# Conv module of a streaming encoder: 35 packs of taps on TensorE for 31, and another order of the steps

## The chip, the cores and the metric

The kernel runs on one core of a Trainium2 chip. The metric is the device time of one execution, in microseconds (us). Before the change three runs took 2794.42, 2795.19 (the median) and 2796.18 us.

In the views of the profile, PE is TensorE's matmuls and PEld its weight loads, DVE is VectorE, ACT is ScalarE, POOL is GpSimd, and SP is the engine whose queue issues nearly all DMAs (SPq in rows).

## The reference

One inference step of an encoder of four layers, for a prompt of 512 rows and a sample of 64, 1024 channels. Each layer has a token mixer and then a convolutional feed-forward part; the mixer of layer 1 is the convolution module, and only there does the change lie.

```python
def _dwconv(xp, w, b):
    y = lax.conv_general_dilated(xp, w[:, None, :], (1,), 'VALID',
                                 dimension_numbers=('NWC', 'WIO', 'NWC'),
                                 feature_group_count=xp.shape[-1])
    return y + b

def _conv_module(h, state, w_pw1, b_pw1, w_dw, b_dw, ln_g, ln_b, w_pw2, b_pw2):
    a, g = jnp.split(h @ w_pw1 + b_pw1, 2, axis=-1)
    glu = a * jax.nn.sigmoid(g)
    xp = jnp.concatenate([state, glu], axis=1)
    c = jax.nn.silu(_layernorm(_dwconv(xp, w_dw, b_dw), ln_g, ln_b))
    return c @ w_pw2 + b_pw2, xp[:, -(CONV_WIDTH - 1):]

# in _trunk, for layer i:
#   x = x + _rmsnorm(y, g[1])              y of the mixer
#   y, s = _conv_ffn(h, st, ...)           ConvFFN: up, conv of width 3, gate, down
```

`CONV_WIDTH` is 31: each channel of the depthwise convolution is a sum of 31 shifted rows, each with a weight of its own (a tap).

## The kernel before, in words

Channels lie on the partitions, in eight tiles of 128; the 576 rows of prompt and sample lie along the free axis. A pointwise product is done as three passes of PE (high part by high part, high by low, low by high; lines 287 to 289), so each weight is loaded by SP (512 KB), cast by ACT (L256) and its low part made by DVE (`v_w_l`, L259). Rows are worked on in two parts, `hf` 0 and 1, of 256 and 320 columns.

In the module each tile goes through these steps. PE makes the four products of pw1 (`v_p`, two for the values and two for the gate). DVE turns them into scaled rows (`v_t`, L1320), ACT takes the sigmoid, DVE gates (`v_glu`, L1329). Then the 31 taps: a number of them in packs of four on PE, one on ACT (L1394), the rest on DVE, one instruction over 128x606 each (`v_cv`, L1396). For the packs the tile's gated rows are first copied to four tiles `v_g` (L1374), one for each group of 32 channels, with the four shifts beside each other; DVE makes diagonal weights (`v_dg`, L1381); and a pack is eight matmuls (L1405, 16 records in the trace) into two cuts of 256 and 350 columns. Three matmuls close the sum with the mean `v_about` (L1412 to 1414). The join (`v_d`, L1421) adds the two parts on DVE; ACT squares; PE sums rows and squares over the channels (`v_sums`, L1450). Behind the last sums come the statistics and the second pointwise product (pw2), whose weights are loaded in the stage too.

`CPACKS` gives the packs of each tile. The order of ACT, DVE, POOL and PE in the stage is written out by hand in the string `CORDER`: each word is a step and a tile, and a third sign repeats it. `do()` plays the words in turn:

- x: a quarter of a tile's product; t, i, g: turn, sigmoid, gate;
- C: the four copies; y: diagonals; e: one pack; w: the closing matmuls;
- b: the first tap outside the packs, on ACT; d: one tap on DVE; j: the join; z, q: squares and sums;
- H, h, l: load, cast and low part of a pw1 weight; W, O, o: the same for pw2;
- R: steps of the input's norm; r, v: state rows; m, n, u: centring; K: a table of ACT.

SP is not in the string. Its order is set by the scheduler, from when the buffers of its loads come free.

The constants of the module come in earlier, while the feed-forward part of layer 0 ends: `columns` (L200 to 227) loads rows by SP to a stage tile, transposes them on PE and copies them from PSUM by ACT. Among them are the packs' columns, 32 small loads. Where the loads stand in SP's order, other loads wait behind them, such as `f_d`, the down-projection's weights of that feed-forward part.

Of the kernel before, what the change touches and what calls it, by code (L numbers as in the profile page):

```python
# [17 lines left out]
P = 128  # L18
# [5 lines left out]
NF = 22  # L24
NEG = -1.0e30
APART = 1
CPACKS = (5, 4, 4, 4, 4, 4, 3, 3)

CORDER = (
# [8 lines left out]
)  # L38

AORDER = (  # L40
# [92 lines left out]
def encoder_step_kernel(  # L133
# [12 lines left out]
    V, S, G, T = nc.vector, nc.scalar, nc.gpsimd, nc.tensor  # L146

    def pool(name, bufs=1, **kw):
        return ctx.enter_context(tc.tile_pool(name=name, bufs=bufs, **kw))
# [6 lines left out]
    wp = pool("work", 6)  # L156
# [11 lines left out]
    def ms_tile(name):  # L168
        return msp.tile([P, 512], F32, tag="ms", name=name)
# [10 lines left out]
    def w_tile(name, shape, dt=F32):  # L180
        return wp.tile(shape, dt, tag="t", name=name)

    def dram(ap, off, dims):
        return bass.AP(ap.tensor, ap.offset + off, dims)
# [14 lines left out]
    def columns(name, pieces, n, tile_pool=None, tag="ct", bufs=2):  # L199

        pt = ms_tile(f"{name}_ps")
        ct = (tile_pool or sp).tile([P, n], F32, tag=tag, bufs=bufs, name=name)
        at, group, used, stage = 0, [], 0, None
        cuts = []
        for src, rows in pieces:
            done = 0
            while done < rows:
                take = min(rows - done, P - used)
                cuts.append((src, done, take, at, used))
                done += take  # L210
                used += take
                if used == P:
                    at, used = at + P, 0
        starts = sorted({c[3] for c in cuts})
        for a in starts:
            stage = w_tile(f"{name}_r{a}", [P, P])
            m = 0
            for src, done, take, at_, used_ in cuts:
                if at_ == a:
                    to = stage[used_ : used_ + take]  # L220
                    if len(src.shape) == 3:
                        to = to.rearrange("r (a b) -> r a b", a=src.shape[1])
                    nc.sync.dma_start(to, src[done : done + take])
                    m = max(m, used_ + take)
            T.transpose(pt[:, a : a + m], stage[:m], ident[:m, :m])
        S.copy(ct, pt[:, :n])
        return ct
# [1044 lines left out]
    def conv_module(i, j):  # L1272
        n = f"v{i}"
        rows = lambda a, k: (a[j].rearrange("(c p) -> c p", p=P), k)

        packs, at = [], 296
        four = {}
        for c, np_ in enumerate(CPACKS):
            four[c] = at
            for q in range(4):  # L1280
                at += np_
                packs.append((dram(conv_w_dw[j], c * P + q * 32, [[4 * D, np_], [D, 4], [1, 32]]), np_))
        ct = columns(f"{n}_ct", [rows(conv_b_pw1, 16), rows(conv_b_dw, 8), rows(conv_ln_g, 8), rows(conv_ln_b, 8), rows(conv_b_pw2, 8), (conv_w_dw[j].rearrange("w (c p) -> (w c) p", p=P), 248), *packs], at)
        wt = ct[:, 48:296].rearrange("p (w c) -> p w c", c=8)

        pm = w_tile(f"{n}_pm", [P, P])
        V.tensor_copy(pm.rearrange("p (r s) -> p r s", s=4), ident.rearrange("p (s r) -> p r s", s=4))
        pps = ms_tile(f"{n}_tp_ps")
        T.matmul(pps[:, : at - 296], pm, ct[:, 296:at], start=True, stop=True)
        tp = sp.tile([P, at - 296], F32, tag="tp", bufs=1, name=f"{n}_tp")  # L1290
        S.copy(tp, pps[:, : at - 296])
        stt = columns(f"{n}_st", [(state_conv[j, 0].rearrange("w (c p) -> (w c) p", p=P), 240)], 240, tag="mix").rearrange("p (w c) -> p w c", c=8)
# [58 lines left out]
        class Tile:  # L1351
# [4 lines left out]
            def __init__(self, c):  # L1356
                self.c = c
                self.m = f"{n}_{c}"
                self.packs = CPACKS[c]
                self.te = 4 * self.packs  # L1360
# [71 lines left out]
            def rows(self):  # L1432
                c, pt = self.c, self.pt
                S.copy(po[c // 2][:, :, (c % 2) * P : (c % 2 + 1) * P], pt[:30, : 2 * P].rearrange("p (a b) -> p a b", a=2))
                if c % 2:
                    for s, dst in ((0, p_conv), (1, s_conv)):
                        nc.sync.dma_start(dst[j, 0][:, (c // 2) * 256 : (c // 2 + 1) * 256], po[c // 2][:, s])
# [410 lines left out]
    for at, i in enumerate(layers):  # L1848
        mixer = (attention, conv_module, chunk_mlp)[i % 3]
        subs += [mixer(i, i // 3, *(True,) * (at == 0)), ffn(i)]  # L1850
# [57 lines left out]
```

## Time and profile before

| | |
|---|---|
| runs, median | 2795.19 us (2794.42 to 2796.18) |
| profiled execution | 2793.36 us, span 2791.6 us |
| granted clock of TensorE, mean | 0.990 |
| PE, DVE, ACT, POOL busy in the span | 98%, 67%, 41%, 14% |
| the stage of the string, 694.00 to 844.30 us | 150.30 us: PE 134.45, DVE 147.16, ACT 39.66 |

The page counts busy time over the whole span, whereas windows cut it at stated times. A timeline row is a start, a duration, an engine, a line, and the operation with what it writes and reads; x4 means four alike in a row. In brackets stands the idle time of the engine ahead of it and what released it. The clock in a window is the granted share of full speed.

### The profile page before, as it was taken

The numbers are of one execution on the slowest core, as the hardware profiler recorded it, in microseconds if no ns is written. First come the engines' busy times: TensorE is split into PE (matmuls) and PEld (weight loads), VectorE is DVE, ScalarE is ACT, GpSimd is POOL, SyncE is SP. The second block draws the span as 40 slices with busy tenths as digits, with TensorE's granted clock in tenths as the row PEclk, the third lists the DMA queues.
The fourth block names the chain that finished last, engine by engine and source line by source line (L and its number), as shares of the span: only waits on it lengthen the run. The fifth ranks groups of instructions, "written<-read, shape, count | busy, mean of one in ns | idle before, by whom it ended". The sixth has DMA issues, their size and how long they took to land.

```text
span 2791.6 us, 52728 instructions
## 1 busy us (share of the span) xinstructions
PE 2740.8 (98%) x20825; PEld 2622.4 (94%) x20825; DVE 1858.2 (67%) x4199; ACT 1137.2 (41%) x2393; POOL 386.9 (14%) x937
## 2 busy tenths in 40 slices
PE   8999999998998999999999999999999999999998
PEld 7889999998867999999999999999999879999998
DVE  5668666666994866666747657666676676766674
ACT  4655433334225543333434224432334664533243
POOL 3122111110000111111002102211110121211111
PEclk9999999999998999999999999999999999999999
DMA  6312322222641232322223221322222421322221
GB/s 166 91 48 69 99 78 90 76 64 64 151 113 40 63 105 76 90 78 92 75 80 97 78 76 55 92 84 84 82 90 61 107 57 40 106 76 86 81 84 59
DMA packets 357625, 230.69 MB, mean 83 GB/s; under 512 B 43038, under 2 KB 347906, under 8 KB 357250
## 3 DMA queue, kind: packets, MB, share of 16 engines
q1 hardware_dynamic: 357378, 227.33, 28.5%
q8 instruction: 164, 2.69, 0.4%
q14 instruction: 83, 0.68, 0.1%
HBM read 212.87 MB, written 7.45 MB: 79 GB/s over the span
## 4 chain that ended last, share of the span: by engine, by line
PE 90%; DVE 7%; DMA 1%; issue 1%; ACT 1%; SPq 0%; POOL 0%; POOLq 0%; DVEq 0%; ACTq 0%
PE f_p L287 13%; PE f_p L289 13%; PE f_p L288 13%; PE o_p L287 10%; PE o_p L288 10%; PE o_p L289 10%; DVE v_cv L1396 3%; PE m_u_p L287 1%; PE m_u_p L289 1%; PE m_u_p L288 1%; PE m_vp L287 1%; PE m_vp L288 1%; PE m_vp L289 1%; PE t_o L1178 1%; PE t_sp L1117 1%; PE t_qp L287 1%
## 5 line engine op out<-in xcount | busy, mean ns | idle before, releaser
L287 PE MATMUL f_p<-n_hi,f_w_h 128*128 128x320 f32 (+1 forms) x2688 | 799.8, 298 | 0.0
L289 PE MATMUL f_p<-n_hi,f_w_l 128*128 128x320 f32 (+1 forms) x2688 | 798.0, 297 | 0.0
L288 PE MATMUL f_p<-n_lo,f_w_h 128*128 128x320 f32 (+1 forms) x2688 | 797.9, 297 | 0.0
L287 PEld LDWEIGHTS f_p<-n_hi,f_w_h 128*128 128x128 f32 x2688 | 510.4, 190 | 4.5 <-issue 4.1
L288 PEld LDWEIGHTS f_p<-n_lo,f_w_h 128*128 128x128 f32 x2688 | 510.4, 190 | 0.0
L289 PEld LDWEIGHTS f_p<-n_hi,f_w_l 128*128 128x128 f32 x2688 | 510.4, 190 | 0.0
L287 PE MATMUL o_p<-f_ah,f_d_h 128*128 128x256 f32 (+1 forms) x1408 | 419.6, 298 | 2.2 <-ACT f_d_h L256 2.2
L288 PE MATMUL o_p<-f_al,f_d_h 128*128 128x256 f32 (+1 forms) x1408 | 418.5, 297 | 0.0
L289 PE MATMUL o_p<-f_ah,f_d_l 128*128 128x256 f32 (+1 forms) x1408 | 417.6, 297 | 0.0
L256 ACT CAST f_w_h<-f_w_f 128x512 fp32r<-128x512 f32 x352 | 200.8, 618 | 494.9 <-PE f_p L288 235.6
L537 DVE TENSOR_TENSOR o_y<-o_p,o_y 128x256 f32<-128x256 f32 (+1 forms) x432 | 195.1, 455 | 262.0 <-PE o_p L289 260.7
L800 DVE TENSOR_TENSOR f_ub<-f_p,n_R 128x256 f32<-128x256 f32 x352 | 148.3, 423 | 286.9 <-PE f_p L289 282.3
L287 PEld LDWEIGHTS o_p<-f_ah,f_d_h 128*128 128x128 f32 x1408 | 268.5, 191 | 4.0 <-ACT f_d_h L256 2.5
L288 PEld LDWEIGHTS o_p<-f_al,f_d_h 128*128 128x128 f32 x1408 | 268.6, 191 | 0.2 <-issue 0.2
L289 PEld LDWEIGHTS o_p<-f_ah,f_d_l 128*128 128x128 f32 x1408 | 268.3, 191 | 0.2 <-issue 0.2
L259 DVE TENSOR_TENSOR f_w_l<-f_w_f,f_w_h 128x512 fp32r<-128x512 f32 x352 | 229.1, 689 | 20.0 <-ACT f_w_h L256 17.9
L256 ACT CAST f_d_h<-f_d_f 128x512 fp32r<-128x512 f32 x176 | 101.3, 619 | 232.6 <-PE f_p L288 171.8
L808 POOL COPY f_fo<-f_ub 128x2 f32<-128x2 f32 x176 | 47.2, 268 | 885.7 <-DVE f_ub L800 878.8
L812 DVE SCALAR_TENSOR_TENSOR f_c<-f_ub,f_ct,f_c 128x578 f32<-128x578 f32 x176 | 144.0, 821 | 38.3 <-ACT f_c L811 38.3
L811 ACT ACTIVATE f_c<-f_ub,f_ct 128x578 f32<-128x578 f32 x176 | 150.8, 863 | 1.4 <-POOL f_fo L808 0.7
L821 ACT CAST f_ah<-f_a 128x576 fp32r<-128x576 f32 x88 | 59.2, 673 | 218.2 <-DVE f_a L818 218.2
L813 DVE SCALAR_TENSOR_TENSOR f_c<-f_ub,f_ct,f_c 128x578 f32<-128x578 f32 x176 | 143.5, 817 | 2.8
(380 smaller groups left out, 5607.6 us busy)
## 6 DMA issues: line engine op xcount, KB each, us to landing
f_w_f<-in_ffn_w_up_dram SPq DMA_DIRECT2D x176, 512.0 KB
f_d_f<-in_ffn_w_down_dram SPq DMA_DIRECT2D x80, 512.0 KB
v_w_f<-in_conv_w_pw_dram SPq DMA_DIRECT2D x24, 512.0 KB
t_wq_f<-in_attn_w_qkv_dram SPq DMA_DIRECT2D x32, 256.0 KB
t_wo_f<-in_attn_w_o_dram SPq DMA_DIRECT2D x32, 256.0 KB
m_wv_f<-in_cmlp_w_in_dram SPq DMA_DIRECT2D x16, 512.0 KB
m_u_w_f<-in_cmlp_w_in_dram SPq DMA_DIRECT2D x16, 512.0 KB
m_wo_f<-in_cmlp_w_out_dram SPq DMA_DIRECT2D x16, 512.0 KB
```

Of the source, the lines that this page charges most:

```text
L256: S.copy(hi[:, a:e], st[:, a:e])
L259: eng.tensor_tensor(lo[:, a:e], st[:, a:e], hi[:, a:e].bitcast(F32), ALU.subtract)
L287: T.matmul(ps, lh, rh, start=(i == 0), stop=False)
L288: T.matmul(ps, lh, rl, start=False, stop=False)
L289: T.matmul(ps, ll, rh, start=False, stop=(i == n - 1))
L537: V.tensor_tensor(ys, ps, ys, ALU.add)
L800: V.tensor_tensor(ub[q][:, b : b + 256], ps[q]()[:, :256], h.R[:, hf * 256 : hf * 256 + 256], ALU.mult)
L811: S.activation(y, ub[q][:, 2:580], AF.Identity, bias=ct[:, 3, c : c + 1], scale=ct[:, 2, c : c + 1])
L812: V.scalar_tensor_tensor(y, ub[q][:, 1:579], ct[:, 1, c : c + 1], y, ALU.mult, ALU.add)
L813: V.scalar_tensor_tensor(y, ub[q][:, 0:578], ct[:, 0, c : c + 1], y, ALU.mult, ALU.add)
L821: S.copy(a_hi[p], am)
L1396: V.scalar_tensor_tensor(self.cv, g, w, self.cv, ALU.mult, ALU.add)
```

## The change

- `CPACKS` becomes (5,5,5,4,4,4,4,4), which sums to 35, in place of (5,4,4,4,4,4,3,3), which sums to 31. Tiles 1, 2, 6 and 7 get one pack more, and four taps fewer on DVE: 100 in all in place of 116.
- `CORDER` is another string with the same steps except for these numbers.
- The columns of the packs no longer lie in the tile `v_ct`, which shrinks from 420 to 296 columns, but in a tile `v_ctp` of their own, 140 columns, from the work pool. There are three and two transposes in place of four, and one more copy on ACT.

```diff
-CPACKS = (5, 4, 4, 4, 4, 4, 3, 3)
+CPACKS = (5, 5, 5, 4, 4, 4, 4, 4)
 CORDER = (
...
-    "e5 o1 d4 w5 b6 y6 d6 e4 W3 j5 e4 d6 z5 d6 w4 d6 C6 d6 x7 j4 d6 z4 d6 x7 d63 x7 d6 t7 d6 i7 g7 d6 x7 O2 d64 e6 O3 t7 d6 "
-    "i7 e6 g7 o2 b7 e6 o2 d7 q4 C7 d7 w6 d7 r7 d7 r6 d7 q5 v6 j6 v7 d7 z6 d7 q6 d76 e7 d72 e7 d7 e7 d72 w7 o32 j7 z7 q7 K0"
+    "x7 O1 y7 W2 t6 o1 i6 o1 e5 g6 W3 e5 b6 d6 e5 d6 e5 d6 w5 C6 d62 x7 j5 d6 z5 d6 x7 t7 d6 i7 g7 d62 x7 O2 d6 o22 d6 e6 "
+    "O3 t7 e6 d6 i7 o3 e6 o3 e6 g7 d6 b7 w6 C7 d7 q3 d7 r7 d7 r6 q5 d7 v6 v7 d77 e7 d72 e7 d7 e7 j6 e7 z6 w7 q6 j7 z7 q7 K0"
 )
...
-        ct = columns(f"{n}_ct", [rows(conv_b_pw1, 16), rows(conv_b_dw, 8), rows(conv_ln_g, 8), rows(conv_ln_b, 8), rows(conv_b_pw2, 8), (conv_w_dw[j].rearrange("w (c p) -> (w c) p", p=P), 248), *packs], at)
+        ct = columns(f"{n}_ct", [rows(conv_b_pw1, 16), rows(conv_b_dw, 8), rows(conv_ln_g, 8), rows(conv_ln_b, 8), rows(conv_b_pw2, 8), (conv_w_dw[j].rearrange("w (c p) -> (w c) p", p=P), 248)], 296)
+        ctp = columns(f"{n}_ctp", packs, at - 296, wp, "t", None)
...
-        T.matmul(pps[:, : at - 296], pm, ct[:, 296:at], start=True, stop=True)
+        T.matmul(pps[:, : at - 296], pm, ctp, start=True, stop=True)
```

On SP, where the module's constants are loaded, stood before (`v_ct_r` are the stage tiles of the columns, `v_st_r` the state's rows, `f_d_4_f` and `f_d_6_f` weights of the feed-forward part):

```order
L223 DMA v_ct_r_7582<-in_conv_w_dw_dram 5x4x32 x4
L223 DMA v_ct_r_7582<-in_conv_w_dw_dram 4x4x32 x17
L223 DMA v_ct_r_7606<-in_conv_w_dw_dram 4x4x32 x3
L223 DMA v_ct_r_7606<-in_conv_w_dw_dram 3x4x32 x8
L223 DMA v_st_r_7628<-in_state_conv_dram 128x128
L223 DMA v_st_r_7631<-in_state_conv_dram 112x128
L277 DMA f_d_4_f<-in_ffn_w_down_dram 128x4x256
L277 DMA f_d_6_f<-in_ffn_w_down_dram 128x4x256
```

and stands now:

```order
L223 DMA v_ctp_r_7588<-in_conv_w_dw_dram 5x4x32 x12
L223 DMA v_ctp_r_7588<-in_conv_w_dw_dram 4x4x32 x17
L223 DMA v_ctp_r_7619<-in_conv_w_dw_dram 4x4x32 x3
L277 DMA f_d_4_f<-in_ffn_w_down_dram 128x4x256
L277 DMA f_d_6_f<-in_ffn_w_down_dram 128x4x256
L223 DMA v_st_r_7633<-in_state_conv_dram 128x128
L223 DMA v_st_r_7636<-in_state_conv_dram 112x128
```

The two loads of the state moved behind the two weight loads; the packs' loads are as many as before.

On DVE at the end of the stage, from the second turn of tile 7 on, stood before:

```order
L1320 TENSOR_TENSOR v_7_t_9796<-v_7_p_9715,n_0_R 128x320
L1320 TENSOR_TENSOR v_7_t_9798<-v_7_p_9749,n_0_R 128x320
L1396 SCALAR_TENSOR_TENSOR v_6_cv<-v_6_glu,v_ct,v_6_cv 128x606
L1329 SCALAR_TENSOR_TENSOR v_7_glu<-v_7_t_9796,v_ct,v_7_t_9798 128x256
L1329 SCALAR_TENSOR_TENSOR v_7_glu<-v_7_t_9796,v_ct,v_7_t_9798 128x64
L259 TENSOR_TENSOR v_w_l<-v_w_f,v_w_h 128x512 x2
L1396 SCALAR_TENSOR_TENSOR v_7_cv<-v_7_glu,v_ct,v_7_cv 128x606 x5
L1421 TENSOR_TENSOR v_6_d<-v_6_pc_9782,v_6_cv 128x256
L1421 TENSOR_TENSOR v_6_d<-v_6_pc_9783,v_6_cv 128x256
L1421 TENSOR_TENSOR v_6_d<-v_6_pc_9783,v_6_cv 128x64
L1396 SCALAR_TENSOR_TENSOR v_7_cv<-v_7_glu,v_ct,v_7_cv 128x606 x13
L259 TENSOR_TENSOR v_w_l<-v_w_f,v_w_h 128x512 x2
```

and stands now:

```order
L1321 TENSOR_TENSOR v_7_t_9806<-v_7_p_9725,n_0_R 128x320
L1321 TENSOR_TENSOR v_7_t_9808<-v_7_p_9759,n_0_R 128x320
L1397 SCALAR_TENSOR_TENSOR v_6_cv<-v_6_glu,v_ct,v_6_cv 128x606
L259 TENSOR_TENSOR v_w_l<-v_w_f,v_w_h 128x512 x2
L1330 SCALAR_TENSOR_TENSOR v_7_glu<-v_7_t_9806,v_ct,v_7_t_9808 128x256
L1330 SCALAR_TENSOR_TENSOR v_7_glu<-v_7_t_9806,v_ct,v_7_t_9808 128x64
L1397 SCALAR_TENSOR_TENSOR v_6_cv<-v_6_glu,v_ct,v_6_cv 128x606
L1397 SCALAR_TENSOR_TENSOR v_7_cv<-v_7_glu,v_ct,v_7_cv 128x606 x14
L1422 TENSOR_TENSOR v_6_d<-v_6_pc_9792,v_6_cv 128x256
L1422 TENSOR_TENSOR v_6_d<-v_6_pc_9793,v_6_cv 128x256
```

The last low parts of pw2 (`v_w_l`) moved from the end to a place ahead of tile 7's gate, the join of tile 6 moved behind all taps, and 14 taps of tile 7 stand where 18 stood.

On SP beside it stood before (`v_7_g` are the copies for tile 7's packs, `v_w_f` the next weights of pw2):

```order
L1374 DMA v_7_g_9829<-v_7_glu 128x1x614
L1374 DMA v_7_g_9830<-v_7_glu 128x1x614
L1374 DMA v_7_g_9831<-v_7_glu 128x1x614
L1374 DMA v_7_g_9832<-v_7_glu 128x1x614
L1437 DMA out_dram<-v_po_9846 30x256 x2
L277 DMA v_w_f<-in_conv_w_pw_dram 128x8x128 x2
```

and stands now:

```order
L277 DMA v_w_f<-in_conv_w_pw_dram 128x8x128 x2
L1375 DMA v_7_g_9846<-v_7_glu 128x1x618
L1375 DMA v_7_g_9847<-v_7_glu 128x1x618
L1375 DMA v_7_g_9848<-v_7_glu 128x1x618
L1375 DMA v_7_g_9849<-v_7_glu 128x1x618
L1438 DMA out_dram<-v_po_9864 30x256 x2
```

The two weight loads moved ahead of the copies. Outside the preparation and the stage all engines keep their order.

## Rows read from the trace of the kernel before

**Rows 1.** Busy time, share of the span and instructions, from the page's first part.

```profile
PE 2740.8 (98%) x20825; PEld 2622.4 (94%) x20825; DVE 1858.2 (67%) x4199; ACT 1137.2 (41%) x2393; POOL 386.9 (14%) x937
```

**Rows 2.** Windows of the stage: stretch, length, busy by engine, clock, DMA share, GB/s.

```profile
694.00:844.30 150.30, 134.45 (x1191) 107.11 (x1192) 147.16 (x243) 39.66 (x72) 1.71 (x8) 0.95 0.49 123
...
700.26:818.69 118.43, 117.10 (x1050) 97.46 (x1054) 116.17 (x190) 31.87 (x59) 1.71 (x8) 0.99 0.55 139
...
825.82:830.49 4.67, 0.01 (x2) 0.01 (x1) 4.53 (x7) 0.26 (x1) 0.00 (x0) 0.93 0.92 167
830.49:836.50 6.01, 5.89 (x39) 3.41 (x43) 5.80 (x9) 0.68 (x1) 0.00 (x0) 0.50 0.63 177
...
843.90:861.00 17.10, 11.28 (x46) 8.20 (x47) 10.37 (x47) 8.47 (x16) 0.00 (x0) 0.51 0.11 31
```

**Rows 3.** DVE's groups by form, 694 to 844.3: count, busy us, mean ns, idle before.

```profile
L1396 DVE SCALAR_TENSOR_TENSOR v_cv<-v_glu,v_ct,v_cv 128x606 f32<-128x606 f32 x116 | 98.3, 848 | 3.0
L259 DVE TENSOR_TENSOR v_w_l<-v_w_f,v_w_h 128x512 fp32r<-128x512 f32 x32 | 20.6, 686 | 0.0
```

**Rows 4.** Timeline of DVE at the stage's end: start us, duration us, work.

```profile
822.34 0.88 DVE L1320 TENSOR_TENSOR v_t<-v_p,n_R 128x320 f32<-128x320 f32 x2
...
823.91 0.68 DVE L1329 SCALAR_TENSOR_TENSOR v_glu<-v_t,v_ct,v_t 128x256 f32<-128x256 f32 x2
...
825.71 4.39 DVE L1396 SCALAR_TENSOR_TENSOR v_cv<-v_glu,v_ct,v_cv 128x606 f32<-128x606 f32 x5
...
830.81 11.47 DVE L1396 SCALAR_TENSOR_TENSOR v_cv<-v_glu,v_ct,v_cv 128x606 f32<-128x606 f32 x13
842.20 1.29 DVE L259 TENSOR_TENSOR v_w_l<-v_w_f,v_w_h 128x512 fp32r<-128x512 f32 x2
843.40 0.88 DVE L1421 TENSOR_TENSOR v_d<-v_pc,v_cv 128x256 f32<-128x256 f32 x3
```

**Rows 5.** Timeline of PE: nine packs, the last product, tile 7's packs and closing.

```profile
714.60 0.31 PE L289 MATMUL v_p<-n_hi,v_w_l 128*128 128x320 f32 x1
714.83 9.39 PE L1405 MATMUL v_pc<-v_g,v_dg 128*32 128x256 f32 x144
...
818.38 0.31 PE L289 MATMUL v_p<-n_hi,v_w_l 128*128 128x320 f32 x1
...
832.52 5.79 PE L1405 MATMUL v_pc<-v_g,v_dg 128*32 128x256 f32 x46
838.24 0.70 PE L1412 MATMUL v_pc<-v_about,ident 128*128 128x256 f32 x2
...
839.21 0.33 PE L1414 MATMUL v_pc<-v_about,ident 128*128 128x64 f32 x2
```

**Rows 6.** Timeline of SP's issues in the preparation.

```profile
601.96 26.07 SPq L223 DMA_DIRECT2D v_ct_r<-in_conv_w_dw_dram  x35
628.14 0.86 SPq L223 DMA_DIRECT2D v_st_r<-in_state_conv_dram  x2
629.09 0.94 SPq L277 DMA_DIRECT2D f_d_f<-in_ffn_w_down_dram  x2
```

**Rows 7.** Timelines of ACT and of PE behind those loads, with idle time and releaser.

```profile
633.11 1.14 ACT L256 CAST f_d_h<-f_d_f 128x512 fp32r<-128x512 f32 x2 [1.16 <-DMA f_d_f<-in_ffn_w_down_dram]
...
633.78 0.58 PE L287 MATMUL o_p<-f_ah,f_d_h 128*128 128x256 f32 x1 [2.23 <-ACT f_d_h L256]
```

**Rows 8.** Windows of the same stretch.

```profile
630.00:634.00 4.00, 0.92 (x5) 0.69 (x6) 0.71 (x2) 2.26 (x6) 1.12 (x3) 0.74 0.86 267
634.00:639.00 5.00, 5.00 (x25) 5.00 (x26) 2.77 (x5) 1.40 (x4) 0.00 (x0) 0.53 0.45 127
```

**Rows 9.** Timeline of SP's issues at the stage's end.

```profile
824.73 4.97 SPq L1374 DMA_DIRECT2D v_g<-v_glu  x4
...
832.06 0.40 SPq L277 DMA_DIRECT2D v_w_f<-in_conv_w_pw_dram  x1
...
843.51 0.40 SPq L277 DMA_DIRECT2D v_w_f<-in_conv_w_pw_dram  x1
```

12 rows, old and new, of the table CORDER are left out of this document.

## The prediction

> **What bounds the kernel now.** I read the engine shares first [rows 1]: TensorE (PE) is busy 2740.8 of 2791.6 us, VectorE (DVE) 67%. By this share alone a change that moves work from DVE to PE should lose. The share is an average, though, so I cut the table of windows at the ends of the stage that the change rewrites [rows 2]. In 694.00 to 844.30 us the picture turns: DVE is busy 147.16 of 150.30 us, PE 134.45. The PE idle time sits in one place: from 825.82 to 830.49 PE does nothing (0.01 us), and from 830.49 to 836.50 it works at a granted clock of 0.50, the 1.2 GHz level. But in the 118.43 us up to the last pointwise product both engines are full: PE 117.10, DVE 116.17. So DVE sets the end of the stage, and PE is close behind it; at most 1.33 us of PE idle time lies in that long part.
>
> The groups of DVE by form [rows 3] show what it does: 116 taps `v_cv`, 98.3 us. The timeline of DVE at the end of the stage [rows 4] is dense from the turn of tile 7 (822.34) to the join of tile 7 (843.40); 13 taps there take 11.47 us, 0.882 us each from start to start. The timeline of PE [rows 5] gives the other side: nine packs take 9.39 us (144 records, 16 to a pack, 1.04 us each) at full clock, and the last pointwise product starts at 818.38 and ends by 818.69. PE is then 3.65 us ahead of the DVE turn that reads it.
>
> **The change part by part.**
>
> *Preparation.* SP issues 35 column loads in 26.07 us before [rows 6] and as many after: 32 of them are for the packs in both, and each fetches at most two rows more. What moves is the two `v_st_r` loads, which stood ahead of `f_d_4_f` and `f_d_6_f` and now stand behind. SP spends 628.14 to 629.09 on them [rows 6], so the two weight loads leave 0.95 us earlier. PE waits for their first half: its product at 633.78 has 2.23 us of idle time put down to the cast of `f_d`, and that cast at 633.11 has 1.16 us put down to the load [rows 7]. The whole 0.95 us is on the path; the transposes of `v_st` go to the middle of products that are dense anyway, and the one more ACT copy lies in the same wait. Bounds: 0 if the transfer was limited by what flew before it, -3 if the clock stays up as well (it is 0.53 for the 5 us after that wait [rows 8], which costs some 2.3). I take **-0.95**.
>
> *Work moved.* 4 packs more, 16 taps fewer: DVE loses 16 x 0.882 = 14.1 us and gets wider diagonals, at most 0.5 us; PE gets 4 x 1.04 = 4.2 us. Which of these counts is decided by where they stand. Before the last product of tile 7 the new order has 27 packs instead of 25, and the other PE work there is the same set (24 quarter products, six state transposes, four rounds of sums, two closings, the centre). So that product ends at 818.69 + 2.1, less what the 1.33 us of waits gives back: 819.5 to 820.8, I take 820.1. DVE has 13 taps fewer and two `v_w_l` more (1.3 us by [rows 3]: 20.6/32 each) ahead of the turn of tile 7: it would be there at 822.34 - 11.5 + 1.3 + 0.5 = 812.6. It must wait for PE some 7.5 us. Thus only 822.34 - 820.1 = 2.2 us of the 11.5 appear at this point; PE is late next.
>
> *From the turn to the copies.* Turn, one tap and gate of tile 7 took 2.25 us before (822.34 to 823.91 + 0.68 = 824.59 [rows 4]); two `v_w_l` (1.29) now stand between them: the gate ends at 820.1 + 3.5 = 823.6. The four copies that PE needs for tile 7's packs follow it on SP. Before, the packs run as a block from 832.52 [rows 5], 7.9 us after the gate; the copies' issue alone is 4.97 us [rows 9]. That gives 831.5.
>
> *A wait that is added.* The two pw2 weight loads that were issued after the copies, at 832.06 and 843.51 [rows 9], now stand ahead of them on SP, and the second needs a stage buffer that the two `v_w_l` just before the gate set free. Queued behind it are the four copies, and behind those tile 7's packs on PE. Two loads of the same size moved 267 GB/s over 630 to 634 [rows 8], while the window of the copies already has a DMA share of 0.92 [rows 2]. Bounds for the delay: 0 if the first load is through and the second small beside the copies, and 1.9 us for one load of 512 KB at 267 GB/s entirely in front. I take 0.5, nearer the lower end because the first load's buffer is free long before.
>
> The window of the copies shows the engines shared at 0.92. The Trainium skill ("DMA: Bandwidth & Descriptors", section "Two DMAs through the same engine are not ordered") says that within one queue of one DMA engine descriptors start in order, though they need not finish so. By that rule the copies start behind the load, the delay is the whole 1.9 and the time 2793.0; no row here shows a load directly ahead of such copies. The sum does not use it.
>
> *Tile 7's packs.* PE starts them at 832.0 after an idle time like the one before (4.67 us, after which the clock was 0.50 for 6.01 us [rows 2]). The 46 recorded of 48 matmuls took 5.72 us from 832.52 to 838.24, so three packs take 5.97. The fourth costs 1.04 at the full clock or 1.99 at the pace of these three; I take 1.5. The three closing matmuls take 1.3 (838.24 to 839.54). End: 832.0 + 5.97 + 1.5 + 1.3 = 840.8; with both ends of the delay and of the fourth pack 839.8 to 842.7.
>
> *The join.* DVE, after the gate, has 15 taps (13.2) and tile 6's join (0.8): 837.6. The pw2 lows that stood before the last join (842.20 [rows 4]) are gone from there. So the join of tile 7 starts at 840.8 on PE's account, not at 843.40: **-2.6**. Behind it square, sums, table load and statistics stand in the old order, so all later work shifts by this; the sums of tile 6, now after tile 7's packs, fill PE in the join's 0.9 us and cost nothing.
>
> *Sum.* -0.95 - 2.6 = -3.55. The profiled execution took 2793.36 (span 2791.6), 1.83 below the runs' median of 2795.19. From the median: **2791.6**.
>
> **The rivals.**
>
> *A, the forecast:* the tail ends on copies, then four packs at a partly low clock. 2789.6 to 2794 with its bounds. Chance 0.50.
>
> *B, the clock holds or the copies are early.* If PE idles only some 3.5 us before tile 7's packs and is not slowed, they end at 831.5 + 4.2 + 1.3 = 837.0 and DVE's 837.6 decides: -5.8. PE would also be busy up to the last sums, and the statistics stretch after 843.90, at 0.51 before [rows 2], might run faster: 11.28 us busy there, of which I allow up to 3. -0.95 - 5.8 = 2788.4, down to 2785.4. For it: PE's idle time before the packs is shorter than before. Against it: PE's wait of 2.23 us before 633.78, behind sparse work, also ended at a low clock [rows 7, 8]. 0.28.
>
> *C, PE is not the bound.* If the 117.10 us of PE hides slack (records whose ends are modelled), all 14.1 us of DVE come out: 2795.19 - 14.1 + 0.5 - 0.95 = 2780.6. Against it: nine packs in a row run at one rate, and the first of them follows the product before it without a gap [rows 5]. 0.08.
>
> *D, the other side: one PE gap in the middle.* The place is tile 5's packs. In the new order they stand after the first quarter of tile 7's products and need PSUM banks that the second turn of tile 6 on DVE frees; counting durations of these groups along the new order, PE is there at 801.4 and DVE at 800.9, both estimates. If DVE is late there by more than the 2.2 us that the stage gains, PE stops as it does at 825.82. A gap of that size costs 4.67, and 6.01 us at half clock behind it 3.0: +7.7, and the time is 2791.6 + 7.7 = 2799.3. It decides from a gap of about 2 us with its slow restart. For it: PE is now the bound, so nothing absorbs a gap. Against it: DVE has lost work everywhere ahead of that point. 0.14.
>
> That the packs' columns come late is no case of its own: they are made some 60 us ahead of the stage.
>
> **How the numbers follow.** A change below 0.2%, 5.6 us, cannot be told from none here. Below 2789.6 lie C (0.08), most of B (0.24) and the lower edge of A (0.06): faster 0.38. Above 2800.8 lies the upper half of D: 0.07. The rest, 0.55, is the same. The range reaches down through most of B and up into D, leaving C and D's upper part out: 2785.5 to 2797.0. A's own range is 2789.6 to 2794.
>
> **What would show it.** Right: 100 taps on DVE; DVE idle for several us before the second turn of tile 7, waiting for PE; the last `v_p` about 1.4 us later than before, relative to the stage's start; PE idle before tile 7's packs with copies as what it waits for; the join waiting for PE; PE's wait for `f_d` shorter by about 1 us. Wrong: any new PE gap over 1 us before the last `v_p` (D); DVE without a wait at tile 7's turn (C); tile 7's packs at 1.04 us each throughout (B); the copies' landing more than 10 us after the gate, which would make the added loads the story.

## The result

The changed kernel took 2758.93 us in the median of four runs (2755.92 to 2763.33), the kernel before 2794.9 (2794.42 to 2796.18): ratio 0.9875, 95% interval 0.9864 to 0.9887, 36 us faster. I had forecast 2791.6, with a range of 2785.5 to 2797.0; the prediction was wrong, in size by a factor of ten. The profiled execution took 2759.21 us (span 2757.3).

The shares of the page after, against [rows 1]: DVE loses 13.5 us, as 16 taps should give; but PE, to which work was added, loses 28.3.

```profile
PE 2712.5 (98%) x20890; PEld 2596.1 (94%) x20890; DVE 1844.7 (67%) x4183; ACT 1137.7 (41%) x2394; POOL 381.8 (14%) x937
```

That row alone says that something outside the change's own stage got quicker. To see where, I set the same instruction of both traces side by side. PE's `v_both_t`, just behind the stage, before and after:

```profile
847.26 0.48 PE L1572 MATMUL v_both_t<-ident,v_both 128*128 128x128 f32 x1 [0.92 <-ACT v_both L1569]
```

```profile
834.46 0.33 PE L1573 MATMUL v_both_t<-ident,v_both 128*128 128x128 f32 x1 [1.46 <-ACT v_both L1570]
```

Up to there the changed kernel gained 12.8 us. The first diagonals of the stage start at 693.96 and 690.41: 3.5 of these us were gained ahead of the stage, 9.3 in it. The other 21.5 (of 34.3 between the spans of the two profiled executions) are gained behind it, where nothing was moved. They come evenly: in the feed-forward parts the changed kernel runs ahead by 0.64 us more in every 77, ahead of the stage as well as behind it.

Timeline of PE in a feed-forward part, 24 products of 256 columns from the first row's start to the second's, before and then after:

```profile
1104.97 0.28 PE L287 MATMUL f_p<-n_hi,f_w_h 128*128 128x256 f32 x1
...
1107.85 0.28 PE L287 MATMUL f_p<-n_hi,f_w_h 128*128 128x256 f32 x1
```

```profile
1091.00 0.28 PE L287 MATMUL f_p<-n_hi,f_w_h 128*128 128x256 f32 x1
...
1093.82 0.28 PE L287 MATMUL f_p<-n_hi,f_w_h 128*128 128x256 f32 x1
```

2.88 us before, 2.82 after, that is 120.0 and 117.5 ns from one product to the next. Over the whole trace the mean step (from the start of a 256-column instruction to the start of the next, over some 9,520 that follow each other without a wait) went from 119.68 to 116.71 ns: 2.97 ns each, 28.3 us in all. The 320-column ones stayed (146.71 and 146.67). The clock is at its upper level in both.

The stage by windows (stretch, length, busy by engine PE, PEld, DVE, ACT, POOL, clock, DMA share, GB/s), against [rows 2]; the first row is as long as the one of before and reaches past the stage's end, which now lies near 831:

```profile
690.40:840.50 150.10, 137.53 (x1273) 109.31 (x1273) 137.29 (x243) 42.64 (x77) 1.30 (x8) 0.97 0.50 127
813.40:820.70 7.30, 7.30 (x90) 3.57 (x90) 6.93 (x11) 2.99 (x6) 0.00 (x0) 1.00 0.70 198
820.70:825.01 4.31, 1.87 (x8) 0.41 (x6) 4.13 (x6) 0.00 (x0) 0.00 (x0) 1.00 0.74 206
825.01:830.51 5.50, 5.50 (x65) 3.86 (x66) 5.32 (x9) 0.00 (x0) 0.00 (x0) 1.00 0.00 0
830.50:847.50 17.00, 10.29 (x52) 7.74 (x52) 10.56 (x49) 8.80 (x17) 0.00 (x0) 0.70 0.00 1
```

The long idle window of before, and the low clock behind it, are gone: from 820.70 to 825.01 PE works 1.87 us and the clock stays at 1.00, and the block of tile 7's packs behind it runs at full clock. The timelines of DVE and PE there, against [rows 4] and [rows 5]:

```profile
812.37 0.48 DVE L1321 TENSOR_TENSOR v_t<-v_p,n_R 128x320 f32<-128x320 f32 x1
813.41 0.49 DVE L1321 TENSOR_TENSOR v_t<-v_p,n_R 128x320 f32<-128x320 f32 x1 [0.56 <-PE v_p L289]
...
815.78 0.67 DVE L1330 SCALAR_TENSOR_TENSOR v_glu<-v_t,v_ct,v_t 128x256 f32<-128x256 f32 x2
...
817.47 12.37 DVE L1397 SCALAR_TENSOR_TENSOR v_cv<-v_glu,v_ct,v_cv 128x606 f32<-128x606 f32 x14 [0.25 <-ACT v_cv L1395]
829.75 1.67 DVE L1422 TENSOR_TENSOR v_d<-v_pc,v_cv 128x256 f32<-128x256 f32 x6
```

```profile
813.30 4.29 PE L1406 MATMUL v_pc<-v_g,v_dg 128*32 128x256 f32 x64
...
821.04 0.62 PE L1406 MATMUL v_pc<-v_g,v_dg 128*32 128x256 f32 x2 [0.33 <-DMA v_g<-v_glu]
822.49 0.62 PE L1406 MATMUL v_pc<-v_g,v_dg 128*32 128x256 f32 x2 [0.83 <-DMA v_g<-v_glu]
823.26 0.62 PE L1406 MATMUL v_pc<-v_g,v_dg 128*32 128x256 f32 x2 [0.15 <-DMA v_g<-v_glu]
825.01 4.27 PE L1406 MATMUL v_pc<-v_g,v_dg 128*32 128x256 f32 x58 [1.13 <-DMA v_g<-v_glu]
...
830.18 0.33 PE L1415 MATMUL v_pc<-v_about,ident 128*128 128x64 f32 x2
```

DVE waited 0.56 us at the second turn of tile 7, not 7.5. PE takes the first pack's matmuls one group of channels at a time, as each copy lands. Both joins run when the last tap is done, from 829.75; tile 7's starts at 830.55, just as PE's closing matmuls have ended (830.51), so the two engines meet there.

### The profile page after: what moved, and what is told of

Its sections match the earlier page's. It is cut to its first block, busy times and chain, and to the rows that moved or that the text cites. A ratio compares the mean times of both kernels' runs of the same rounds, so it can differ in the third digit from the quotient of the medians.

```text
span 2757.3 us, 52839 instructions
## 1 busy us (share of the span) xinstructions
PE 2712.5 (98%) x20890; PEld 2596.1 (94%) x20890; DVE 1844.7 (67%) x4183; ACT 1137.7 (41%) x2394; POOL 381.8 (14%) x937
## 4 chain that ended last, share of the span: by engine, by line
PE 94%; DVE 3%; DMA 1%; ACT 1%; issue 1%; SPq 0%; POOL 0%; POOLq 0%; ACTq 0%; DVEq 0%
PE f_p L287 13%; PE f_p L288 13%; PE f_p L289 13%; PE o_p L287 10%; PE o_p L288 10%; PE o_p L289 10%; PE m_u_p L287 1%; PE m_u_p L288 1%; PE m_vp L287 1%; PE m_u_p L289 1%; PE m_vp L288 1%; PE m_vp L289 1%; PE t_o L1178 1%; PE t_sp L1117 1%; PE t_qp L287 1%; PE v_p L287 1%
## 5 line engine op out<-in xcount | busy, mean ns | idle before, releaser
L288 PEld LDWEIGHTS f_p<-n_lo,f_w_h 128*128 128x128 f32 x2688 | 504.8, 188 | 0.0
L259 DVE TENSOR_TENSOR f_w_l<-f_w_f,f_w_h 128x512 fp32r<-128x512 f32 x352 | 228.8, 688 | 20.3 <-ACT f_w_h L256 17.5
```

The costliest lines, as they stand in the source:

```text
L259: eng.tensor_tensor(lo[:, a:e], st[:, a:e], hi[:, a:e].bitcast(F32), ALU.subtract)
L288: T.matmul(ps, lh, rl, start=False, stop=False)
```

## Experiments

Two theories stood at first for the 28 us: that the place of the weights in SBUF did it, or that the new order did. In the program as built the change moves the tiles of the weights, since the column tile `v_ct` ahead of them shrinks: the high parts start at byte 196448 of a partition before, at 195488 after (the buffers follow each other at 4096, so one offset holds for all). In 512 bytes that is 352 before and 416 after. The rows that move against them stay at 96 or 352 in 512.

**b_shift: the kernel before, weights 64 bytes further.**

```diff
-tp = sp.tile([P, at - 296], F32, tag="tp", ...)
+tp = sp.tile([P, at - 280], F32, tag="tp", ...)[:, : at - 296]
```

> The kernel before, with one tile of the small pool 16 columns wider, so that the weight tiles behind it (stage, high and low parts) lie 64 bytes further: their offset in 128 bytes goes from 96 to 32, as in the changed kernel. No instruction and no order differs. Theory P (place of the weights): the products of 256 columns follow each other every 117 ns in place of 120, 9515 of them save 28 us, and the time is 2795 - 28 = 2767 (2763 to 2771). Theory R (the new order, or that run's clock, is what made PE faster): 120 ns and 2795 within 2.

2767.14 us, ratio 0.9904 (0.9889 to 0.9919); mean step 116.57 ns, 320 columns 146.65. PE's timeline, 24 products in 2.82 us:

```profile
1096.53 0.28 PE L287 MATMUL f_p<-n_hi,f_w_h 128*128 128x256 f32 x1
...
1099.35 0.28 PE L287 MATMUL f_p<-n_hi,f_w_h 128*128 128x256 f32 x1
```

The old instructions in the old order are 28 us faster for 64 bytes of padding. Theory R fell.

**a_shift: the changed kernel, the same padding**, by the same edit; its weights lie at 480.

> The changed kernel, with the same tile 16 columns wider: the weights' offset in 128 bytes goes from 32 back to 96. Theory P: pitch 120 ns, 2759 + 28 = 2787 (2783 to 2791); what then remains against the kernel before, about 8 us, is the stage and the preparation. Theory R: 117 ns, 2759 within 4.

2776.46 us (0.9936; 0.9922 to 0.9951), the step 118.55 ns: some six tenths of the loss that theory P in its form of 128 bytes said (1.84 of 3 ns; 17.5 of 28 us against the changed kernel). PE's timeline, 24 products in 2.84 us:

```profile
1093.99 0.28 PE L287 MATMUL f_p<-n_hi,f_w_h 128*128 128x256 f32 x1
...
1096.83 0.28 PE L287 MATMUL f_p<-n_hi,f_w_h 128*128 128x256 f32 x1
```

So 480 is not 352 again, though both leave 96 in 128 bytes: a miss that called for a longer period or for another quantity.

**a_four: the changed kernel, four offsets at once.**

```diff
-hi = whp.tile([P, 1024], F32R, tag="wh", ...)
-lo = wlp.tile([P, 1024], F32R, tag="wl", ...)
+hi = whp.tile([P, 1032], F32R, tag="wh", ...)
+lo = wlp.tile([P, 1032], F32R, tag="wl", ...)
```

> The changed kernel with the tiles of high and low parts 8 columns wider, so that the four buffers of each lie at offsets 32, 64, 96 and 0 in 128 bytes. Theory P, in the form that only the offset in 128 bytes counts: the 256-column products of the buffer at 96 take 120 ns, those at 32 117, and the trace gives 0 and 64 their pitch; the time lies between 2759 and 2787, near 2770. Theory P2 (the offset in 64 bytes counts, or the distance between stage and weights): all four alike, or two and two. Theory R: all 117 and 2759.

2763.76 us (0.9893; 0.9873 to 0.9913). With each record put to its buffer, the step was 114.5 ns for high parts at 416, 118.8 at 448, 118.5 at 480 and 119.0 at 0. The offset of the weights alone does not order them: low parts at 64 took 116.8. What does is the distance from the current product's moving rows to the next product's weights. Where it is 64 or 192 in 256 bytes the means are 114.5 to 115.8 ns; at all other distances 117.8 to 119.8. This gave theory D. Nearly all moving rows of this kernel lie at 96 in 256, so this trace alone cannot tell the distance from the place of the next product's weights; the next two kernels were built to.

**b_all64: the kernel before, weights and moving rows both 64 bytes further.**

```diff
-thirty2 = cp.tile([P, 1], F32, tag="thirty2", name="thirty2")
+thirty2 = cp.tile([P, 24], F32, tag="thirty2", name="thirty2")[:, :1]
```

> The kernel before, with a tile of the const pool wider, so that both the weights and the rows that move against them lie 64 bytes further: the weights at 416 in 512 bytes as in the changed kernel, the moving rows at 160 or 416 in place of 96 or 352; their distance stays 0 in 128 bytes. Theory D (the distance of the two places decides): pitch 120 ns, 2795 within 3. Theory P (the place of the weights alone decides): 116.6 ns and 2767 within 3.

2794.41 us, ratio 0.9999 (0.9990 to 1.0009), step 119.68 ns. PE's timeline, 24 products in 2.88 us:

```profile
1106.47 0.28 PE L287 MATMUL f_p<-n_hi,f_w_h 128*128 128x256 f32 x1
...
1109.35 0.28 PE L287 MATMUL f_p<-n_hi,f_w_h 128*128 128x256 f32 x1
```

The weights lie where b_shift has them, and nothing is gained: the place of the weights alone is out.

**b_rows64: only the moving rows 64 bytes further** (the edit of b_all64 on b_prep, below, and 112 columns behind `tp` that put the weights back to 352).

> b_prep (the old order, 31 packs) with the moving rows alone 64 bytes further, at 160 or 416 in 512 bytes; the weights are put back to 352 in 512 bytes, where the kernel before has them. Theory D (the distance of weights and moving rows decides, 64 in 128 bytes is quick): 116.6 ns in place of 119.7, 2794 - 28 = 2766 within 3. Theory P (weights at 352 are slow wherever the rows lie): 119.7 ns, 2794 within 2.

2771.15 us (0.9917; 0.9900 to 0.9933), step 117.29 ns. The time is 5 us over the expected 2766, outside its margin; the direction is theory D's. PE's timeline, 2.82 us:

```profile
1099.82 0.28 PE L287 MATMUL f_p<-n_hi,f_w_h 128*128 128x256 f32 x1
...
1102.64 0.28 PE L287 MATMUL f_p<-n_hi,f_w_h 128*128 128x256 f32 x1
```

Sorted within each trace by distance in 256 bytes, weights less rows (products of lines 287 to 289 alone), the steps at the main offset of each kernel give: 0, 119.9 ns (before, b_all64); 64, 116.5 to 116.7 (b_shift, after, a_all32); 128, 118.6 (a_shift); 192, 117.7 (b_rows64). The slower 192 fits the 5 us missed (0.72 ns over b_shift's mean on 9,520 steps is 6.9). About a tenth of the steps in some kernels lie at a second distance, and one trace orders them the same way: in the changed kernel 828 steps at 192 took 117.9 ns beside 116.6 for 7,674 at 64, in b_rows64 821 at 64 took 114.3 beside 117.7 for 7,699 at 192. That it is a distance and not a place is shown from both sides.

**a_all32: the changed kernel, all tiles 32 bytes further**, by `cp.tile([P, 16], ...)` for `thirty2`: starts at multiples of 64, the distance as in the changed kernel.

> The changed kernel, all tiles behind the const pool 32 bytes further: the weights at 448 in 512 bytes, the moving rows at 128 or 384, so both at multiples of 64; the distance stays 64 in 128 bytes. Theory D: as the changed kernel, 116.7 ns and 2759 within 4. Theory P: in a_four the weights at 448 took 118 to 119 ns, so 2759 + 9515 x 1.6 ns = 2774. A third theory, that starts at multiples of 64 are read faster: below 2755.

2758.72 us, ratio 0.9872 (0.9858 to 0.9887), step 116.83 ns: theory D again. It is level with the changed kernel, no better; the third theory fell.

**b_prep: the preparation alone**, on the old order and 31 packs; the weights stay at 352.

```diff
-CPACKS = (5, 5, 5, 4, 4, 4, 4, 4)   and the new CORDER
+CPACKS = (5, 4, 4, 4, 4, 4, 3, 3)   and the old CORDER
```

> The kernel before, with the preparation alone changed: the packs' columns (still 31 packs, the old order) in a tile of the work pool. The weights stay at offset 96. Theory P: pitch 120 ns, the wait of PE for f_d is 1 us shorter, 2795 - 1 = 2794 (2792 to 2795). Theory Q (the preparation itself, by other places of its tiles, makes the products faster): 2767.

2793.79 us beside 2793.71 (ratio 0.9998; 0.9988 to 1.0007). The time does not resolve 1 us; the wait can be read in the trace. PE's product behind it:

```profile
633.93 0.58 PE L287 MATMUL o_p<-f_ah,f_d_h 128*128 128x256 f32 x1 [1.67 <-ACT f_d_h L256]
```

The wait is 1.67 us, 2.23 before [rows 7]. From the last product ahead of the columns to this one it is 3.6 us; with the old preparation 4.65, 4.8 and 5.7 (before, b_all64, b_shift), with the new one 3.4 to 4.0 in seven other kernels. In b_prep's one trace the gain does not reach the end of the stage: the first diagonals start 0.3 us earlier than before, the last join 0.7 later.

**a_31: the new order with 31 packs**, the weights where the changed kernel has them (the tile `tp` is padded for that).

```diff
-CPACKS = (5, 5, 5, 4, 4, 4, 4, 4)
+CPACKS = (5, 4, 4, 4, 4, 4, 3, 3)
 # CORDER: one e less and four d more in tiles 1, 2, 6 and 7
```

> The changed kernel's order with the packs of before, 31: one pack less and four taps more on DVE in tiles 1, 2, 6 and 7; the weights stay where the changed kernel has them. Theory V (DVE sets the stage's end in both, so the taps count): 16 taps of 0.88 less the DVE's idle time of some 4 us, 2759 + 10 = 2769. Theory O (the order made the gain, not the packs): 2759 within 3.

2770.47 us (0.9913; 0.9896 to 0.9929), theory V within 2. DVE's timeline of the tail: all taps behind the gate run in one block, 23 of them, and only then the joins.

```profile
819.75 0.67 DVE L1331 SCALAR_TENSOR_TENSOR v_glu<-v_t,v_ct,v_t 128x256 f32<-128x256 f32 x2
820.34 20.20 DVE L1398 SCALAR_TENSOR_TENSOR v_cv<-v_glu,v_ct,v_cv 128x606 f32<-128x606 f32 x23
840.46 1.67 DVE L1423 TENSOR_TENSOR v_d<-v_pc,v_cv 128x256 f32<-128x256 f32 x6
```

DVE's waits in that stage are three kinds, 3.3 us in all; in the changed kernel 4.2. DVE sets the end in both. From the first diagonals to the last join the stage is 149.4 us before and in b_shift, 152.4 here, 140.1 in the changed kernel: the four packs are worth 12.3, and the new order, with 31 packs as a_31 places them, costs 3.

**a_q6: the changed kernel, with tile 6's join and sums ahead of tile 7's packs.**

```diff
-"... q5 d7 v6 v7 d77 e7 d72 e7 d7 e7 j6 e7 z6 w7 q6 j7 z7 q7 K0"
+"... q5 d7 v6 v7 d76 j6 d7 z6 q6 e7 d72 e7 d7 e7 e7 w7 j7 z7 q7 K0"
```

> The changed kernel, with tile 6's join moved ahead of the last taps on DVE and its sums ahead of tile 7's packs on PE, as they stood before. PE then stops at those sums until about 825 and cannot take tile 7's packs as their copies land. Theory H (that stop let the clock fall before; its absence is where the tail's gain is from): granted clock 0.5 during tile 7's packs, which end some 3 to 4 us later, 2759 + 3.5 = 2762.5. Theory N (the copies set the packs' start, the order does not matter): the packs end within 0.8 us, 2759.

2761.43 us (0.9882; 0.9867 to 0.9897), against 2758.72 of a_all32 on the same occasion and 2758.93 of the changed kernel on another, near theory H. Windows of PE from the end of tile 6's packs on, and PE's timeline:

```profile
816.36:821.10 4.74, 1.90 (x21) 0.55 (x20) 4.56 (x6) 0.63 (x2) 0.00 (x0) 0.99 0.95 234
821.10:827.90 6.80, 3.56 (x26) 2.14 (x30) 6.59 (x11) 0.68 (x1) 0.00 (x0) 0.50 0.18 47
827.90:833.00 5.10, 5.10 (x61) 3.81 (x53) 0.90 (x3) 0.00 (x0) 0.00 (x0) 1.00 0.00 0
```

```profile
824.23 1.06 PE L1451 MATMUL v_sums<-v_d,ones 128*32 128x256 f32 x2 [5.97 <-DVE v_d L1422]
...
826.26 5.15 PE L1406 MATMUL v_pc<-v_g,v_dg 128*32 128x256 f32 x62
```

PE stops 5.97 us at the sums and the clock is at 0.50 for the 6.80 that follow 821.10: through the sums and the first 1.6 us of tile 7's packs, whose larger part runs at 1.00. The packs end 4.7 us later than in the changed kernel, counted from the first diagonals, so theory N fell; the stage is 144.2 us long instead of 140.1 (140.1 in a_all32 too). By the completions in the trace the last of the four copies had landed at 823.13, before the sums were released at 824.23. So the wait at the sums is enough for the clock to fall. In the kernel before, PE stood at the same sums:

```profile
830.49 1.06 PE L1450 MATMUL v_sums<-v_d,ones 128*32 128x256 f32 x2 [4.66 <-DVE v_d L1421]
```

The new order does not by itself keep the clock up, though. a_shift has the very order of the changed kernel, and PE takes the first pack there in the same pieces; yet the clock fell during the packs. Windows of a_shift, of the pieces and of the low clock:

```profile
821.97:826.79 4.82, 1.89 (x8) 0.41 (x6) 4.61 (x7) 0.02 (x1) 0.00 (x0) 1.00 0.74 189
827.03:830.44 3.41, 3.41 (x32) 2.44 (x28) 3.27 (x5) 0.00 (x0) 0.00 (x0) 0.50 0.00 0
```

The stage took 142.5 us there, and the join of tile 7 waited for PE. PE's waits for the copies sum to 2.4 us in the changed kernel, 2.7 in a_all32 and 3.0 in a_four, where the clock stayed at 1.00, and to 2.9 in a_shift, where it fell (in a_31, with a pack less, it fell too, for 3.4 us). What decides between them no run here shows.

## Why the prediction was wrong

By medians the 36 us part like this: the distance of weights and rows, 27.8 (before to b_shift); the new order and the preparation with 31 packs, +3.3 (b_shift to a_31); four packs in place of 16 taps, 11.5 (a_31 to after). These kernels were timed on different occasions, each beside the kernel before, so the parts are good to some 2 us.

*The sum* is the step that failed most. It had two terms, and "all later work shifts by this" took every other instruction at its old duration, because its order was unchanged. The order was; the addresses were not. The section on the change even names the tile that shrinks from 420 to 296 columns, and I priced only its loads. The runs showed in its place 2.97 ns less on each of some 9,520 steps, 28 us. No row of before could have given the 3 ns; but that a change in a tile's size moves all tiles behind it could be read from the code, and belonged among the unknown terms of the range.

*Work moved* failed as to the bound. I had PE at 820.1 at the last product (in before's time) and DVE waiting 7.5 us. Relative to the first diagonals, that product started 1.8 us earlier than before, where I had it 1.4 later; in a_shift, with a step of 118.55 ns, 1.0 earlier. I read 117.10 busy of 118.43 as PE's need. It was not: the busy time holds stretched records. By starts, from the first diagonals to that product, the two more packs cost 1.8 us, but the products of pw1 took 2.7 less and the sums 1.2 less, and the quicker step explains only some 0.9 of that (288 products at 2.97 ns). The rest were gaps that went when DVE's taps did: 0.95 us lie between two products from 724.38 on, of which the trace counts 0.68 as idle, and 0.68 and 0.54 around the sums from 779.50 on, where products follow in 0.12 to 0.15. Rival C had that half right, and a_31 shows DVE as the bound under the new order.

*From the turn to the copies* came out by luck. The gate to the packs' block took 8.6 us (816.45 to 825.01) against 7.9 + 0.5, but the 7.9 of before was not the copies' time: PE stood at the sums until 830.49, and by the completions in the trace the last copy landed at 833.46, 8.9 us after the gate and inside the block. In the changed kernel the block waits for the last copy, which landed at 824.97, 8.5 after the gate. SP issued both weight loads ahead of the copies:

```profile
811.72 4.55 SPq L277 DMA_DIRECT2D v_w_f<-in_conv_w_pw_dram  x2
816.54 4.98 SPq L1375 DMA_DIRECT2D v_g<-v_glu  x4
```

*A wait that is added* thus cost nothing that the traces show: the lower of its two bounds. The first load had landed at 815.91; the second was issued at 815.89 and landed at 820.03, the first copy at 821.00. The in-order start of the Trainium skill's page "DMA: Bandwidth & Descriptors" (section "Two DMAs through the same engine are not ordered") would by my working have cost the whole 1.9; this trace shows no delay, though the load did land ahead of the copies.

*Tile 7's packs* failed on the clock. I carried over the idle time of before, which was the wait at the sums and not at copies, and the low clock behind it. Rival B had a clock that holds and the join at DVE's time, which is what this trace shows; that the clock held is in part luck, as a_shift shows. *The join* came on DVE's account, as in rival B: 9.3 us gained in the stage where the forecast had 2.6.

*Preparation* held in size at PE's gap: 1.0 us in b_prep, forecast 0.95; 0.6 in the changed kernel itself (4.65 to 4.04). That it shortens the whole is not shown: b_prep's median is level with the kernel before. The two issues stand in the order foretold:

```profile
625.61 0.96 SPq L277 DMA_DIRECT2D f_d_f<-in_ffn_w_down_dram  x2
626.66 0.93 SPq L223 DMA_DIRECT2D v_st_r<-in_state_conv_dram  x2
```

*Rivals*: D, a PE gap in the middle, did not occur; B was right on the tail alone, and no rival had the quicker step. One count does not close: 0.06 of A stands below 2789.6, where A's own range begins.

## What to carry to other kernels

A diff that resizes a tile moves everything allocated behind it: compare the addresses of operands before and after, and take a step-to-step time of the commonest instruction in a part that was not changed. Where a gain appears everywhere at a steady rate, pad one kernel back by the same bytes before crediting the edit. An instruction that waits at the head of PE's queue costs more than its wait when the clock falls behind it. Putting work ahead of it whose data comes in pieces kept the clock up in three kernels here, but not in all.

## What the runs showed of the hardware

- Consecutive 256-column matmuls, each behind a load of its own 128x128 weights, stood 116.5 to 119.9 ns apart on the mean, by the distance in 256 bytes between the moving rows and the next weights: of 0, 64, 128 and 192 as main offsets, 64 was quickest and 0 slowest. 320-column ones stayed at 146.6 to 146.7 ns in all these kernels. The weights' load overlaps the current product in the trace, which would fit two reads that disturb each other; that is argued, not shown. Nor is it settled whether the next weights or the current ones count (nearly all steps outside a_four have both at one distance), or why steps at 64 fall to 114.3 in b_rows64 and 114.5 in a_four, where they are the minority, while those at 0 in a_four take 117.9.
- In the changed kernel the clock stayed at its upper level through 4.31 us in which PE was busy 1.87, in pieces; in a_shift 4.82 us with 1.89 busy, in like pieces, were followed by 3.41 us at 0.50. In a_q6 it fell within one idle stretch of 5.97 us.
- Four copies of some 310 KB, the first issued 0.65 us behind a load of 512 KB, had all landed 8.5 us after DVE's gate of tile 7 (the changed kernel); without such a load ahead, in the kernel before, it was 8.9.
